# Turning merged rows from tokens to columns: transposes on TensorE, or 32x32 blocks on VectorE and a way through DRAM

## The chip, the cores and the metric

The kernel runs on one core of a Trainium2 chip. The metric is device time in microseconds (us) of one execution of the whole kernel, lower being better. The core has a matrix engine (TensorE, in the profile PE, with its weight loads as PEld), a vector engine (VectorE, DVE), a scalar engine (ScalarE, ACT), a general engine (GpSimd, POOL) and a queue that does little but issue transfers (SyncE, SP). The engines run side by side; each executes its own instructions strictly in the order in which the program emits them, and semaphores make one wait for another.

## What is computed

One layer of a bidirectional encoder: 256 tokens, width 2048, float32.

```python
xn = rms_norm(x, norm_pre_w)
u_lru, g_lru, q, k, v, g_attn, m_lru, m_attn = split(xn @ w_in)
y_a = (rg_lru forward + backward of the convolved u_lru) * silu(g_lru)
y_b = windowed_gqa(rope(q), rope(k), v, sink) * silu(g_attn)
merged = sigmoid(m_lru) * (y_a @ w_proj_a) + sigmoid(m_attn) * (y_b @ w_proj_b)
x = x + rms_norm(merged @ w_out, norm_post_w)
```

The last lines matter here. `merged` is 256 x 2048. The products that make it put tokens on the partitions; the product with `w_out` needs it the other way round, with `merged`'s columns on the partitions, because that is the dimension it sums over. Between the two, `merged` is turned.

## The kernel before

**Precision.** Each float32 operand is split into a high part (fp32r, made by a cast on ScalarE) and a low part (the remainder, made by a subtraction on VectorE), and a product is three matmuls: high by high, high by low, low by high. `split` does so for the weights (ScalarE L219, VectorE L221), `parts_of` for activations (ScalarE L148, and one tick later VectorE L149).

**Weights.** 1 MB of weights is one step: a *quad* (512 output columns by a quarter of the depth), a *block*, or a *part* of a Strassen-like scheme of seven products (class `Seven`; groups L, M, N, A and O). A quad has two halves of twelve matmuls each, a part two halves of six. The order of all steps is written out by hand in the strings `START`, `MERGE` and `OUT`. In `MERGE` the quads `b0.0` to `b3.3` are `y_b @ w_proj_b`, where the first digit is the column block c of 512 columns; in between stand parts of groups A and O. A raw load (SP, L207) goes to one of three ring buffers and is emitted three steps ahead of its matmuls; the cast is emitted four halves ahead and the subtraction three.

**Ticks.** Time in the program's text is counted in ticks: one for each half of a quad and one for a whole part. `soon(fn, d)` puts work d ticks later into the emission order; `at(tick, fn)` puts it at a given tick. Within a tick come the transfers that the step fetches, then the work that is due, then the splits, then the matmuls. So a load that waits on SP, or a subtraction that waits on VectorE, holds up all that was emitted behind it on the same engine.

**The turn.** `add_pb(c)` adds the four quads of column block c. One tick after the last of them `done` runs for both token halves: VectorE multiplies by the gate and adds the other branch (L977, L978), four operations in all. Then `turn(0)` and `turn(1)` (`turn(i)` takes 256 of the 512 columns) follow one and three ticks later. Each has four TensorE transposes of 128x128 into a PSUM bank (L989), a split of the turned bank into the tile `ms` (L148, L149), and `sums_of`, which makes the four sums and differences that the seven-product scheme needs into `mx` (L318 to L326, and another split). `ms` and `mx` are what the `o` quads and the O parts multiply with `w_out`.

**An older turn of the same kind.** The attention probabilities are already turned without TensorE: `head.flip` transposes 32x32 blocks on VectorE (L905), `head.send` writes four groups of 32 partitions to a DRAM tile `turn` with four transfers on SP (L914), and `head.fetch` reads it back with the partition groups in their places (L919), two ticks after the send.

**Memory.** Nearly all tiles are 4 KB per partition and come from one pool of 45 units; a new tile waits until its slot has been left by the tile before.

Of the kernel before, what the change touches and what calls it, by code (L numbers as in the profile page):

```python
# [15 lines left out]
F32 = mybir.dt.float32  # L16
F32R = mybir.dt.float32r
AF = mybir.ActivationFunctionType
ALU = mybir.AluOpType
PSUM = bass.MemoryType.PSUM  # L20

P = 128
# [80 lines left out]
def content(p):  # L103
    if p[0] == "part":
        _, g, a, q = p
        m, c = SEVENS[g]
        b, f = SEVEN[a][2]
        return "part", m, c + (-512 if g == "A" else 512) * f, b, q
    return p


def wall_rows():
    return {k: n for n, k in enumerate(dict.fromkeys(content(p) for p in load_plan()))}


def body(ctx, tc, x, x0, xT, wall, wlru, pvec, npost, ident_d, mask_d, rope_d, out):
    nc = tc.nc
# [5 lines left out]
    dram = ctx.enter_context(tc.tile_pool(name="dram", bufs=1, space=bass.MemoryType.DRAM))  # L123
    ctx.enter_context(tc.manual_schedule())

    def unit(name, dt=F32, shape=(P, 4, S)):
        return units.tile(list(shape), dt, tag="u", name=name)

    def bank(name, shape=(P, 2, S)):
        return psum.tile(list(shape), F32, tag="bg", name=name, bufs=4)  # L130
# [4 lines left out]
    def half_unit(name, tag, dt=F32, bufs=2):  # L135
        return small.tile([P, 2, S], dt, tag=tag, name=name, bufs=bufs)


    def pair_unit(name):
        return unit(name, F32R, (P, 2, 2, S))  # L140
# [6 lines left out]
    def parts_of(h, l, src):  # L147
        nc.scalar.copy(h, src)  # L148
        soon(lambda: nc.vector.tensor_tensor(l, src, h.bitcast(F32), ALU.subtract))  # L149
# [9 lines left out]
    def ticks(i=None):  # L159
        return sum(1 if p[0] == "part" else 2 for p in plan[:len(steps) if i is None else i])  # L160

    def at(hs, fn):
        assert hs >= now[0], (hs, now[0])
        due.setdefault(hs, []).append(fn)
# [9 lines left out]
    def soon(fn, d=1):  # L174
        at(now[0] + d, fn)
# [3 lines left out]
    row = wall_rows()  # L179
    flat = lambda t: t.rearrange("p a b -> p (a b)") if len(t.shape) == 3 else t  # L180

    def raw_tile(i):
        t = ring.tile([P, 2, 1024], F32, tag="raw", name=f"raw{i}", bufs=3)
        raws[i] = [t[:, h] for h in range(2)]
        return t
# [12 lines left out]
    def chained(i):  # L198
        return plan[i][0] == "part" and groups[plan[i][1]].where(plan[i][2]) != "z"

    def fetch(i, lead):
        if i >= len(plan):
            return
        if plan[i][0] == "part":
            groups[plan[i][1]].fetch(plan[i], lead)
        if lead == 3 and i not in raws and not chained(i):
            nc.sync.dma_start(flat(raw_tile(i)), wall[row[content(plan[i])]])  # L207
# [54 lines left out]
    def add_rows(name, act, done, spare=False, last=False):  # L262


        got, held = [], []

        def products(t, g, h, wh, wl):

            for low in range(2):
                for j in range(2):  # L270
                    k = 4 * g + 2 * h + j
                    sl = slice(j * 512, (j + 1) * 512)
                    a = act[k // 2][:, k % 2, :, t * P:(t + 1) * P]
                    for i in range(1 if low else 2):
                        nc.tensor.matmul(got[t], a[:, i], (wl if low else wh)[:, sl], start=k + low + i == 0, stop=low == 1 and k == KT - 1)  # L275

        def half(g, h, wh, wl):
            if g == 0 and h == 0:
                if last:
                    got.extend(banks(f"{name}{t}", (P, 2, 512))[:, 0] for t in range(2))  # L280
                elif spare:
                    got.extend(bank(f"{name}{t}", (P, 512)) for t in range(2))
                else:
                    ps = banks(name, (P, 2, 512))
                    got.extend(ps[:, t] for t in range(2))
            if last and g >= 2:
                products(0, g, h, wh, wl)
                held.append((1, g, h, wh, wl))
            else:
                for t in range(2):  # L290
                    products(t, g, h, wh, wl)
            if g == 3 and h == 1:
                if last:
                    done(0, got[0])
                    for a in held:
                        products(*a)
                    done(1, got[1])
                else:
                    soon(lambda: [done(t, got[t]) for t in range(2)])

        for g in range(4):
            steps.append(("quad", lambda h, wh, wl, g=g: half(g, h, wh, wl)))
# [6 lines left out]
    def sums_of(name, src, done, f=None):  # L309
        a = src.rearrange("p a b -> p (a b)")  # L310
        a11, a12, a21 = (a[:, i * P:(i + 1) * P] for i in (0, 2, 1))
        ends = src.rearrange("p a (b c) -> p (a b) c", b=2)[:, 0:4:3]
        psum = f is None
        f = (half_unit(f"{name}f", "uu", F32) if psum else f).rearrange("p a (b c) -> p (a b) c", b=2)
        t = unit(name, F32R, (P, 4, 2, P))

        def make(a21):
            nc.vector.tensor_tensor(f[:, 0:2], ends, a21.unsqueeze(1).to_broadcast([P, 2, P]), ALU.subtract)  # L318
            nc.vector.scalar_tensor_tensor(f[:, 2], f[:, 1], -1.0, a11, ALU.mult, ALU.subtract)
            nc.vector.scalar_tensor_tensor(f[:, 3], f[:, 2], -1.0, a12, ALU.mult, ALU.subtract)  # L320
            soon(lambda: parts_of(t[:, :, 0], t[:, :, 1], f))
            done(t)

        if psum:

            nc.scalar.copy(f[:, 3], a21)  # L326
            soon(lambda: make(f[:, 3]))
        else:
            make(a21)

    away = [dram.tile([P, 4, 4, 2 * P], F32, name=f"away{q}") for q in range(2)]

    def x_sums(n):
        v = unit(f"xa{n}")
        nc.vector.tensor_tensor(v[:, 0:2], xs[n][:, :, 0].bitcast(F32), xs[n][:, :, 1].bitcast(F32), ALU.add)
        store = lambda t: nc.sync.dma_start(away[n // 4][:, :, n % 4], t.rearrange("p a b c -> p a (b c)").bitcast(F32))
        sums_of(f"xx{n}", v[:, 0:2], lambda t: soon(lambda: store(t), 7), v[:, 2:4])
# [6 lines left out]
    class Seven:  # L346
# [42 lines left out]
        def rows(self, m, q, j):  # L389
            a, n = SEVEN[m][0], 4 * q + j  # L390
            if a[0] == "a":
                t, b = int(a[1]) - 1, int(a[2]) - 1
                src = self.act[n][:, b, :, t * P:(t + 1) * P]
            elif self.sums is None:
                src = self.kept[m, q][:, j]
            else:
                src = self.sums[n][:, SUMS.index(a)]
            return src[:, 0], src[:, 1]
# [355 lines left out]
    tm, sm, ms, msum = {}, {}, {}, {}  # L754
# [219 lines left out]
    def add_pb(c):  # L974
        def done(t, ps):
            g = sm[c][:, t]
            nc.vector.tensor_tensor(g, ps, g, ALU.mult)  # L977
            nc.vector.tensor_tensor(g, tm[c][:, t], g, ALU.add)  # L978
            if t == 1:
                for i in range(2):  # L980
                    soon(lambda i=i: turn(i), 1 + i * (1 if c == 3 else 2))

        def turn(i):

            ps = bank(f"mt{c}{i}")
            for t in range(2):
                for j in range(2):
                    sl = slice((2 * i + j) * P, (2 * i + j + 1) * P)
                    nc.tensor.transpose(ps[:, j, t * P:(t + 1) * P], sm[c][:, t, sl], ident)  # L989
            n = 2 * c + i  # L990
            m = ms[n] = pair_unit(f"ms{n}")
            parts_of(m[:, :, 0], m[:, :, 1], ps)
            sums_of(f"mx{n}", ps, lambda t: msum.update({n: t}))

        add_rows(f"pb{c}_", yb, done)
# [81 lines left out]
    b, n = ticks(), ticks(len(plan))  # L1077
# [159 lines left out]
```

## Time and profile before

| | us |
|---|---|
| median of 3 runs | 877.22 |
| lowest and highest | 876.87, 877.27 |
| the profiled execution | 876.5 |
| its span, first to last instruction | 874.7 |
| TensorE busy in the span | 864.9 |
| VectorE busy | 728.6 |
| ScalarE busy | 643.1 |

The profile is of one execution. Busy time is the time in which an engine executes; a wait is idle time just before an instruction, with the event that ended it. "L" and a number is a line of the kernel. A DMA row tells from the issue on the queue to the landing of the data. Positions are us from the start of the span, and a row of the timeline gives the start, the duration, the engine, the line, and in brackets the idle time before it.

### The profile page before, as it was taken

Reading aid. Unit: us, or ns where it says so; the run is one execution under the profiler, and the core shown is the slowest. Engines: PE = TensorE matmul, PEld = TensorE weight load, DVE = VectorE, ACT = ScalarE, POOL = GpSimd, SP = SyncE. Lnnn points to the kernel's source line nnn. Section 1 sums busy time; section 2 is a strip of 40 time slices with the busy share of each in tenths; the row PEclk is TensorE's granted clock in tenths of the full one; section 3 lists DMA queues with packets and bytes.
Section 4 is the critical chain, followed back from the end, with each engine's and each line's share of the span. In section 5 each row is a group of like instructions: output and inputs, shape, how many; then the busy total and the mean of one; then the engine's idle time right before and its main releaser. Section 6 shows DMA issues by size and latency. Waiting matters only on the chain.

```text
span 874.7 us, 12312 instructions
## 1 busy us (share of the span) xinstructions
PE 864.9 (99%) x4474; PEld 741.7 (85%) x4474; DVE 728.6 (83%) x975; ACT 643.1 (74%) x929; POOL 66.1 (8%) x97
## 2 busy tenths in 40 slices
PE   9999999999999999999999999999999999999996
PEld 8888888888888888888888888888888888888885
DVE  6898999898887989779677788988678778778885
ACT  7689687877888696887777699976567456555654
POOL 0000001012000011100001200000000101000200
PEclk9999999999999999999999999999999999999999
DMA  9757699999959999996999987999989988968772
GB/s 332 276 194 236 202 362 244 361 332 291 336 186 278 319 298 316 302 314 230 277 345 305 303 297 218 333 326 309 303 323 364 297 269 261 315 248 353 188 198 96
DMA packets 63390, 247.92 MB, mean 283 GB/s; under 512 B 6241, under 2 KB 19297, under 8 KB 47841
## 3 DMA queue, kind: packets, MB, share of 16 engines
q1 hardware_dynamic: 52384, 208.59, 64.6%
q0 software_dynamic: 10368, 37.75, 22.2%
q10 hardware_dynamic: 576, 0.79, 0.3%
q8 instruction: 35, 0.57, 0.2%
q14 instruction: 27, 0.21, 0.1%
HBM read 228.24 MB, written 18.87 MB: 283 GB/s over the span
## 4 chain that ended last, share of the span: by engine, by line
PE 94%; issue 3%; DMA 2%; ACT 0%; POOLq 0%; DVE 0%; SPq 0%; ACTq 0%
PE ga L255 7%; PE q L255 7%; PE gl L255 7%; PE u L255 5%; PE Am L410 4%; PE Mm L410 4%; PE Lm L410 4%; PE Nm L410 4%; PE ga L253 3%; PE q L253 3%; PE gl L253 3%; PE Om L410 3%; PE u L253 3%; PE pa__6025 L275 2%; PE pa__5514 L275 2%
## 5 line engine op out<-in xcount | busy, mean ns | idle before, releaser
L221 DVE TENSOR_TENSOR wl<-raw,wh 128x1024 fp32r<-128x1024 f32 (+1 forms) x252 | 299.1, 1203 | 56.5 <-ACT wh L219 43.9
L219 ACT CAST wh<-raw 128x1024 fp32r<-128x1024 f32 (+1 forms) x251 | 253.7, 1036 | 67.5 <-DMA raw<-wall_dram 39.6
L255 PE MATMUL ga<-xs,wh 128*128 128x512 f32 x256 | 63.5, 391 | 0.0
L255 PE MATMUL gl<-xs,wh 128*128 128x512 f32 x256 | 63.4, 391 | 0.0
L255 PE MATMUL q<-xs,wh 128*128 128x512 f32 x256 | 63.2, 391 | 0.0
L255 PEld LDWEIGHTS q<-xs,wh 128*128 128x128 f32 x256 | 47.0, 188 | 9.1
L255 PEld LDWEIGHTS gl<-xs,wh 128*128 128x128 f32 x256 | 47.0, 188 | 9.0
L255 PEld LDWEIGHTS ga<-xs,wh 128*128 128x128 f32 x256 | 46.7, 188 | 8.8
L255 PE MATMUL u<-xs,wh 128*128 128x512 f32 x192 | 47.5, 391 | 0.0
L255 PEld LDWEIGHTS u<-xs,wh 128*128 128x128 f32 x192 | 35.2, 188 | 6.7
L253 PEld LDWEIGHTS q<-xs,wl 128*128 128x128 f32 x256 | 33.2, 191 | 1.2
L253 PE MATMUL q<-xs,wl 128*128 128x256 f32 x256 | 34.0, 283 | 0.0
L253 PEld LDWEIGHTS ga<-xs,wl 128*128 128x128 f32 x256 | 33.0, 191 | 1.2
L253 PEld LDWEIGHTS gl<-xs,wl 128*128 128x128 f32 x256 | 32.8, 191 | 1.2
L253 PE MATMUL ga<-xs,wl 128*128 128x256 f32 x256 | 33.5, 283 | 0.0
L253 PE MATMUL gl<-xs,wl 128*128 128x256 f32 x256 | 33.2, 283 | 0.0
L253 PEld LDWEIGHTS u<-xs,wl 128*128 128x128 f32 x192 | 24.6, 191 | 0.9
L253 PE MATMUL u<-xs,wl 128*128 128x256 f32 x192 | 24.9, 283 | 0.0
L662 DVE SCALAR_TENSOR_TENSOR uu<-upad,pv,uu 128x256 f32<-128x256 f32 x48 | 23.2, 483 | 1.7
L746 ACT ACTIVATE sig<-sg 128x512 f32<-128x512 f32 x16 | 10.2, 635 | 14.1 <-DVE sg L589 14.1
L148 ACT CAST ms<-mt 128x512 fp32r<-128x512 f32 x8 | 4.7, 588 | 20.0 <-PE mt L989 20.0
L230 PE MATMUL gate<-ul,lwl 128*128 128x256 f32 x64 | 18.1, 283 | 0.0
(513 smaller groups left out, 2097.5 us busy)
## 6 DMA issues: line engine op xcount, KB each, us to landing
raw<-wall_dram SPq DMA_DIRECT2D x121, 1024.0 KB, 7.9
lraw<-wlru_dram SPq DMA_DIRECT2D x8, 512.0 KB, 6.3
away<-xx SPq DMA_DIRECT2D x8, 512.0 KB, 8.7
Lm<-away SPq DMA_DIRECT2D x8, 512.0 KB, 11.2
Mm<-away SPq DMA_DIRECT2D x8, 512.0 KB, 13.4
Nm<-away SPq DMA_DIRECT2D x8, 512.0 KB, 14.2
turn<-pt SPq DMA_DIRECT2D x32, 128.0 KB, 4.4
pl<-turn SPq DMA_DIRECT2D x8, 512.0 KB, 7.2
```

The costliest lines, as they stand in the source:

```text
L148: nc.scalar.copy(h, src)
L219: cast(hs, raw)
L221: nc.vector.tensor_tensor(ls, raw, hs.bitcast(F32), ALU.subtract)
L230: nc.tensor.matmul(ps, wl, xh, start=False, stop=stop, skip_group_check=more)
L253: nc.tensor.matmul(ps[:, 1], wl[:, sl], a[:, 0], start=False, stop=False)
L255: nc.tensor.matmul(ps, wh[:, sl], a, start=k == 0, stop=k == KT - 1)
L275: nc.tensor.matmul(got[t], a[:, i], (wl if low else wh)[:, sl], start=k + low + i == 0, stop=low == 1 and k == KT - 1)
L410: nc.tensor.matmul(self.ps[b], a[i], (wl if low else wh)[:, sl], start=fresh and j + low + i == 0, stop=last and j + low == 2, skip_group_ ...
L662: nc.vector.scalar_tensor_tensor(u, up[:, j, tap:tap + S], cw[:, tap:tap + 1], u, ALU.mult, ALU.add)
L746: nc.scalar.activation(sg, dst, AF.Sigmoid)
```

## The change

For column blocks 0, 1 and 2 the turn takes another way; block 3 keeps the transposes, at the delays it had. One tick after `done`, `flip` lets VectorE transpose the merged tile (128 x 1024) in 32x32 blocks. One tick on, `send` issues four transfers on SP, each for 32 partitions, into a DRAM tile. Three ticks after the flip `fetch` reads that tile back, 512 KB, with the partition groups exchanged. Six and seven ticks after the flip, `rows(0)` and `rows(1)` make from it what `turn(0)` and `turn(1)` made: the split into `ms`, and the sums into `mx` by a new function, which takes its operands from the fetched tile in SBUF and needs no copy of `a21`, but four VectorE operations in place of three.

```diff
+    def turned_sums_of(name, src, done):
+
+        f = half_unit(f"{name}f", "uu", F32).rearrange("p a (b c) -> p (a b) c", b=2)
+        t = unit(name, F32R, (P, 4, 2, P))
+        row = [f[:, i].rearrange("p (a x) -> p a x", a=4) for i in range(4)]
+        a11, a21, a12, a22 = (src[:, i // 2, 4 * (i % 2):4 * (i % 2) + 4] for i in range(4))
+        nc.vector.tensor_tensor(row[0], a11, a21, ALU.subtract)
+        nc.vector.tensor_tensor(row[1], a22, a21, ALU.subtract)
+        nc.vector.scalar_tensor_tensor(row[2], row[1], -1.0, a11, ALU.mult, ALU.subtract)
+        nc.vector.scalar_tensor_tensor(row[3], row[2], -1.0, a12, ALU.mult, ALU.subtract)
+        soon(lambda: parts_of(t[:, :, 0], t[:, :, 1], f))
+        done(t)
...
-            if t == 1:
+            if t == 1 and c == 3:
                 for i in range(2):
-                    soon(lambda i=i: turn(i), 1 + i * (1 if c == 3 else 2))
+                    soon(lambda i=i: turn(i), 1 + i)
+            elif t == 1:
+                soon(flip)
+
+        v = {}
+
+        def flip():
+            v["t"] = unit(f"mt{c}", F32, (P, 2, 4, 4, 32))
+            nc.vector.transpose(v["t"].rearrange("p t c k x -> p t k c x"), sm[c].rearrange("p t (k c x) -> p t k c x", k=4, c=4))
+            for d, fn in enumerate((send, None, fetch, None, None, lambda: rows(0), lambda: rows(1)), 1):
+                if fn:
+                    soon(fn, d)
+
+        def send():
+            v["d"] = dram.tile([4, 32, 2, 4, P], F32, name=f"turnm{c}")
+            t = v.pop("t")
+            for a in range(4):
+                nc.sync.dma_start(v["d"][:, :, :, a].rearrange("c i t x -> i t c x"),
+                                  t[a * 32:(a + 1) * 32].rearrange("p t c k x -> p t c (k x)"))
+
+        def fetch():
+            v["u"] = unit(f"mu{c}", F32, (P, 1024))
+            nc.sync.dma_start(v["u"], v["d"].rearrange("c i t a x -> (c i) (t a x)"))
+
+        def rows(i):
+            src = v["u"].rearrange("p (a k x) -> p k a x", a=8, k=4)[:, 2 * i:2 * i + 2]
+            n = 2 * c + i
+            m = ms[n] = pair_unit(f"ms{n}")
+            wide = lambda s: m[:, :, s].rearrange("p k (a x) -> p k a x", a=8)
+            parts_of(wide(0), wide(1), src)
+            turned_sums_of(f"mx{n}", src, lambda t: msum.update({n: t}))
```

## The prediction

> **What bounds the kernel now.** First the page: who is busy, and who stands in the chain that ended last.
>
> ```profile
> PE 864.9 (99%) x4474; PEld 741.7 (85%) x4474; DVE 728.6 (83%) x975; ACT 643.1 (74%) x929; POOL 66.1 (8%) x97
> PE 94%; issue 3%; DMA 2%; ACT 0%; POOLq 0%; DVE 0%; SPq 0%; ACTq 0%
> ```
>
> TensorE is busy throughout and holds 94% of the chain; 99% alone proves little, since ends of matmuls are modelled. So next the chain in order of time, around the turns of column blocks 0, 1 and 2 ("rounds" below).
>
> ```profile
> 696.48 2.72 PE Am L410 x12
> 699.76 5.48 PE pb__6872 L275 x24
> 705.67 2.77 PE Am L410 x12
> 708.44 10.88 PE pb__6872 L275 x48
> ...
> 727.48 2.72 PE Am L410 x12
> 730.76 5.48 PE pb__7124 L275 x24
> 736.67 5.49 PE pb__7124 L275 x24
> 742.16 2.72 PE Am L410 x12
> ...
> 758.48 2.72 PE pb__7337 L275 x12
> 761.76 2.76 PE pb__7337 L275 x12
> 764.51 2.72 PE Am L410 x12
> 767.67 2.77 PE Om L410 x12
> 770.44 5.44 PE pb__7337 L275 x24
> ```
>
> Twelve matmuls take 2.72 us wherever no turn lies between, and the next group starts where the last ended: a tick is 2.72 us, and TensorE waits for nobody. Only the transposes break the pace. From 696.48 to 708.44 are 11.96 us for 48 matmuls, which the row after does in 10.88: 1.08 us. From 727.48 to 742.16 are 14.68 for 60, by the pace 13.60: 1.08. From 758.48 to 770.44 are 11.96 for 48: 1.08. This is what a round's two turns cost the bound engine.
>
> **TensorE's part.** The change takes 24 of 32 transposes from TensorE.
>
> ```profile
> L989 PE MATMUL mt<-ident,sm x16: 270/272/329, 699.0 to 736.4; 128*128 128x128 f32 x16
> L148 ACT CAST ms<-mt x8: 587/588/588, 699.8 to 796.0; 128x512 fp32r<-128x512 f32 x8
> L149 DVE TENSOR_TENSOR ms<-mt,ms x8: 683/684/685, 702.6 to 797.2; 128x512 fp32r<-128x512 f32 x8
> L326 ACT COPY mx0f<-mt x1: 270/270/270, 700.3 to 700.3; 128x128 f32<-128x128 f32 x1
> L318 DVE TENSOR_TENSOR mx0f<-mt,mx0f x1: 415/415/415, 703.2 to 703.2; 128x256 f32<-128x256 f32 x1
> L319 DVE SCALAR_TENSOR_TENSOR mx0f<-mx0f,mt x1: 286/286/286, 703.6 to 703.6; 128x128 f32<-128x128 f32 x1
> ```
>
> I take 3 x 1.08 = 3.24 us, from starts in the chain, not 24 x 0.272 = 6.53 us, the durations: those overlap, and the pace is what the successor feels. [...]
>
> **ScalarE and VectorE, the same work from another place.** A round loses two copies L326 on ScalarE (0.54 us); the casts of the new `rows` are 128x512 as before, so 0.588 each; reading runs of 32 elements is not in the trace and lies between that and a doubling. It costs nothing while ScalarE idles (12.3 us of 20 busy, below). On VectorE the three operations of the sums (0.415, 0.286 and another of 0.286: 0.99) become four of 128x128: 4 x 0.286 = 1.14, at most 4 x 0.415 = 1.66. The remainders L149 stay. New is the flip.
>
> ```profile
> L905 DVE STREAM_TRANSPOSE pt<-p x16: 704/706/712, 516.7 to 646.6; 128x512 f32<-128x512 f32 x16
> L914 SPq DMA_DIRECT2D turn<-pt x32: 575/611/1465, 524.7 to 649.2; - x32
> DMA to landing us min/median/max: 2.5/4.4/9.4
> L919 SPq DMA_DIRECT2D pl<-turn x8: 319/326/327, 530.4 to 657.9; - x8
> DMA to landing us min/median/max: 3.2/7.2/9.3
> ...
> 720.00:740.00 20.00, 20.00 (x93) 16.42 (x93) 17.20 (x24) 12.28 (x16) 3.50 (x4) 1.00 0.77 230
> ```
>
> The flip is twice as wide: 2 x 0.706 = 1.41 us. A round so adds to VectorE 1.41 + 2 x 0.15 = 1.7 us, and 5.1 in all. In the 20 us of the last row VectorE is busy 17.2; it keeps 2.8 in hand there, so by sums this fits. By order it is tighter.
>
> **Round 0: when must the fetch land?**
>
> ```profile
> 701.45 1.22 DVE L221 TENSOR_TENSOR wl<-Ax0b,wh 128x1024 fp32r<-128x1024 f32 x1
> ...
> 716.70 1.23 DVE L221 TENSOR_TENSOR wl<-raw,wh 128x1024 fp32r<-128x1024 f32 x1 [1.32 <-issue]
> ...
> 727.52 0.69 DVE L977 TENSOR_TENSOR sm<-pb__6872,sm 128x512 f32<-128x512 f32 x1 [2.05 <-PE pb__6872 L275]
> 730.18 3.49 DVE L221 TENSOR_TENSOR wl<-raw,wh 128x1024 fp32r<-128x1024 f32 x3
> ```
>
> The flip comes in front of the split at 701.45, the third after `done`, so it ends at 702.9. Four sends at 0.61 put the last issue at 704.7; by the medians it lands 4.4 later, and the fetch 7.2 after that: 716.4. `rows(0)` stands six ticks behind the flip, the tick of the split at 716.70, before which VectorE already idled 1.32: it arrives at 715.4 and stops there until the data are in. Behind it, up to the next `done`, are five low splits (6.1), two sets of sums (2.3), four remainders (2.7) and one combine of part results (0.7): 11.8 us. Then come the four merging operations (2.8) and the low split of b2.0's second half (1.22). TensorE needs that half at 730.76 - 0.56 (transposes: 727.48 + 2.72 to 730.76) - 1.08 + 2.72 + 0.9 (four high matmuls first) = 732.7. Back from there: landing by 716.9. By the medians 0.5 us are in hand; with both maxima (9.4 + 9.3) it is 723.4 and 6.5 late; with both minima 710. I take zero, as the nearest rows are transfers of just this shape and their medians.
>
> **Round 1: the weight loads behind the sends.** On SP, sends and fetch stand between weight loads.
>
> ```profile
> 697.42 0.33 SPq L809 DMA_DIRECT2D sm<-parksm  x1
> 700.42 0.33 SPq L207 DMA_DIRECT2D raw<-wall_dram  x1
> ...
> 727.48 6.55 SPq L207 DMA_DIRECT2D raw<-wall_dram  x3
> ...
> 747.65 5.49 SPq L207 DMA_DIRECT2D raw<-wall_dram  x3
> ...
> DMA to landing us min/median/max: 6.2/10.2/12.9
> ```
>
> The last line is the landing of the three loads at 727.48. They are b2.2, b2.3 and b3.0; the sends go behind the first, the fetch before the second. The flip starts at 730.18 + 2 x 1.16 - 1.08 = 731.4 and ends at 732.8, the last send is issued at 734.7, it lands at 739.1, the fetch goes out, and b2.3 follows at 739.6 instead of about 731. Landed: 749.8 by the 10.2 us of this stretch, which is DMA-busy. b2.3 starts on TensorE at 742.16 - 2.16 + 2.72 + 5.44 + 2.72 = 750.9; with 0.9 as above, and cast (1.04) and split (1.22) before it:
>
> ```profile
> L219 ACT CAST wh<-raw 128x1024 fp32r<-128x1024 f32 (+1 forms) x251 | 253.7, 1036 | 67.5 <-DMA raw<-wall_dram 39.6
> raw<-wall_dram SPq DMA_DIRECT2D x121, 1024.0 KB, 7.9
> ```
>
> needed by 749.5. So 0.3 late by the local median, 2.0 early by the median of all 121 loads (7.9), 3.7 early by the minimum, and with the slowest send and the slowest load (+5.0, +2.7) 8.0 late. I take 0.3.
>
> **Round 2, round 0's loads, and the rest.** In round 2 the sends stand before b3.2's load, the third of those at 747.65. The merge starts at 758.48 - 2.16, the flip ends four operations (2.75), a split (1.22) and 1.41 later at 761.7, the sends are issued by 764.2, then the load, landing at 772.1 by 7.9 or 774.4 by 10.2. b3.2 starts three steps after 767.67, at 778.6 - 3.24 = 775.4, so 774.0 is early enough: between 1.9 in hand and 0.4 late; I take zero, since the sends are then all that waits on SP. In round 0 the load at 700.42 goes out after the sends, at about 705.5; it feeds b1.3, on TensorE at 719.32 + 2.72 - 1.08 = 721.0, so it has 15 us. POOL's accumulating load into Ax0b waits for the split behind the flip: 1.4 us later, for data that Am4.0 takes, ten steps after the part that freed the tile. The two new tiles per round take two of 45 slots, and the four they replace are allocated six ticks later. What TensorE no longer writes, no bank of PSUM has to hold. If these covers are gone, each costs what lands late, one for one.
>
> **Sum.** -3.24 + 0.3 = -2.9 us. The profiled execution took 876.5 (span 874.7 and 1.8 around it) and would take 873.6; it stands 0.7 below the median of the runs, 877.2, so I predict 874.3.
>
> **Rivals.**
> - *The way through DRAM is slow (slower).* b2.3's load waits on SP for the sends' landing, and TensorE waits for b2.3. For: the loads of this stretch took 10.2 in the median, and a send up to 9.4. At the far end 8.0 late: 877.2 - 3.24 + 8.0 = 882.0. It decides from a landing of b2.3 at 749.5 + 3.24 + 1.75 = 754.5 on. Against: by the 7.9 us of all loads b2.3 is 2.0 early, and each wait on SP also leaves the DMA engines more room for what follows. Chance 0.24. [...]
> - *The gain is eaten on VectorE (within 0.2%).* Round 0's fetch lands 1.5 to 5 us after 716.9, and the backlog of 11.8 us reaches TensorE. For: only 0.5 in hand. Against: 2.05 us of idle time before L977. Around 3 late: 877.0. Chance 0.22.
> - *TensorE was not the bound.* Then its holes stay where the transposes were: 877.2. For: weight loads are only 85% busy. [...] Against: the even pace of 2.72 us. Chance 0.04.
>
> **How the numbers follow.** My forecast, a stall of at most 1.5 us in all, has 0.50: 873.8 to 875.5. A kernel within 0.2% (1.75 us) can't be told from no change: faster 0.50, same 0.26 (the second and third rival), slower 0.24. The range of 8 in 10 leaves out half a tenth below 873.5 (less than no stall) and the worst of the slower cases, stalls beyond 6 us: 873.5 to 880.0.
>
> **What the profile of the changed kernel would show.** Right: in the chain, 2.72 us per twelve matmuls without a break from 690 to 789; flips of about 1.4 us; the fetched tiles landing by 716.9 in round 0, b2.3's load by 749.5 in round 1; TensorE with no idle time before a `pb` or Am matmul. Wrong: casts that wait for raw loads, or TensorE waiting for low splits in 715 to 760; or an earlier stage with the same end, which would mean that something in the O stage sets the end. The prediction fails if transfers land slower than their medians in rounds 0 and 1, for there the margins are 0.5 and -0.3 us.

## The result, and the profile after

The changed kernel takes 883.46 us in the median of six runs (881.61 to 884.08), against 877.2 for the kernel before on the same chip: a ratio of 1.0069, 95% interval 1.0056 to 1.0082. It is slower by 6 us where 2.9 less was forecast, and it lies beyond the upper end of the range. The profiled execution took 883.3 us, with a span of 881.6 (before: 874.7).

First the page of the changed kernel: busy times, the engines' shares of the chain that ended last, and the group of ScalarE's casts of weights.

```profile
PE 866.1 (98%) x4450; PEld 741.8 (84%) x4450; DVE 732.1 (83%) x984; ACT 642.2 (73%) x923; POOL 66.1 (7%) x97
...
PE 87%; DMA 5%; DVE 3%; issue 3%; ACT 1%; SPq 0%; POOLq 0%; ACTq 0%; DVEq 0%
...
L219 ACT CAST wh<-raw 128x1024 fp32r<-128x1024 f32 (+1 forms) x251 | 253.8, 1035 | 89.4 <-DMA raw<-wall_dram 59.5
```

The 24 transposes are gone (4474 - 4450), and yet TensorE is not done sooner. Its share of the chain fell from 94% to 87%, and DMA and VectorE took the place. The last row says what came late: of the 89.4 us for which ScalarE stood before a cast of weights, 59.5 were ended by a raw load. The chain in order of time (start, duration, what) shows where:

```profile
735.12 2.12 PE pb__7115 L275 x8
...
737.28 0.09 DVE mt L1002
...
739.50 9.82 DMA turnm<-mt
749.37 0.33 SPq L1016
...
749.80 5.45 DMA raw<-wall_dram
...
755.35 1.05 ACT wh L219
...
756.45 8.52 PE pb__7115 L275 x24
764.97 5.45 PE pb__7335 L275 x24
...
775.03 9.98 DMA raw<-wall_dram
...
798.43 0.70 DVE mg L991
...
799.17 0.44 PE mt L1032 x2
```

Up to 727 the chain stays with TensorE; from there to 735 it runs through VectorE's splits and merges, late out of round 0. Then it runs through round 1 as the rival "the way through DRAM is slow" has it: flip, sends, landing of the sends, fetch, and only then the load of b2.3, its cast, and TensorE. Behind it stand 24 matmuls that take 8.52 us, and the next 24 take 5.45. Further on the chain leaves TensorE again: VectorE's splits at 770, a raw load at 775.03 that goes out behind them, its cast, more work of VectorE. It comes back to TensorE at the transposes of block 3, which wait for the merge on VectorE (L991).

The table of stretches of 20 us shows the same two places (busy time of PE, PEld, DVE, ACT and POOL, then the granted clock, the share of the DMA engines and GB/s):

```profile
740.00:760.00 20.00, 17.10 (x68) 13.74 (x67) 10.55 (x17) 7.24 (x10) 0.87 (x1) 0.89 0.90 265
760.00:780.00 20.00, 20.00 (x85) 16.46 (x84) 17.67 (x20) 11.68 (x14) 1.73 (x2) 0.94 0.95 274
780.00:800.00 20.00, 18.87 (x85) 15.21 (x84) 15.72 (x24) 9.70 (x13) 0.00 (x0) 1.00 1.02 419
```

Before, TensorE had 90 to 93 matmuls in each of these stretches, at a clock of 1.00. After, it has 68 from 740 to 760, with 2.9 us idle, and the granted clock falls to 0.89 and 0.94; from 756 to 762 it is 0.50. So this stall cost twice: TensorE stood, and it then ran at half clock. TensorE's own timeline at that place:

```profile
756.45 2.08 PE L275 MATMUL pb__7115<-wh,yb 128*128 128x512 f32 x4 [2.90 <-ACT wh L219]
...
759.17 1.91 PE L275 MATMUL pb__7115<-wh,yb 128*128 128x512 f32 x4
...
763.44 1.07 PE L275 MATMUL pb__7115<-wh,yb 128*128 128x512 f32 x4
```

Four matmuls take 1.91 where they take 1.07 a little later. The 24 matmuls at 756.45 took 8.52 instead of 5.45: 3.1 us lost on top of the stall of 2.9. With 1.1 us in round 0 and 1.3 at block 3's transposes, TensorE loses 8.4 us after 690. Less the 3.24 us that the transposes cost no longer, 5.2 are explained of the 6.9 by which the two spans differ; about 1.0 of the rest is there before the change begins: the part of group A that started at 696.48 starts at 697.46. That is scatter: in the profiled executions of the kernels here, which do the same work up to there, the first matmul of this part starts anywhere from 696.0 to 697.8.

Last SP's own timeline, which holds what the rest of this document turns on (start, duration to the end of the last of the group, line, and the count):

```profile
703.69 4.14 SPq L1011 DMA_DIRECT2D turnm<-mt  x4
707.95 1.98 SPq L207 DMA_DIRECT2D raw<-wall_dram  x1
...
714.90 0.32 SPq L1016 DMA_DIRECT2D mu<-turnm  x1
...
737.39 2.77 SPq L1011 DMA_DIRECT2D turnm<-mt  x4
749.37 0.33 SPq L1016 DMA_DIRECT2D mu<-turnm  x1
749.80 0.85 SPq L207 DMA_DIRECT2D raw<-wall_dram  x2
...
770.77 2.55 SPq L1011 DMA_DIRECT2D turnm<-mt  x4
773.42 0.56 SPq L207 DMA_DIRECT2D raw<-wall_dram  x1
```

In each round a weight load goes out right behind the sends or the fetch. The loads that the kernel before issued at 700.42, about 731 and about 753 go out at 707.95, 749.80 and 773.42.

### The profile page after: what moved, and what is told of

It reads as the page before. It is cut to its first block, busy times and chain, and to the rows that moved or that the text cites. A ratio compares the mean times of both kernels' runs of the same rounds, so it can differ in the third digit from the quotient of the medians.

```text
span 881.6 us, 12291 instructions
## 1 busy us (share of the span) xinstructions
PE 866.1 (98%) x4450; PEld 741.8 (84%) x4450; DVE 732.1 (83%) x984; ACT 642.2 (73%) x923; POOL 66.1 (7%) x97
## 4 chain that ended last, share of the span: by engine, by line
PE 87%; DMA 5%; DVE 3%; issue 3%; ACT 1%; SPq 0%; POOLq 0%; ACTq 0%; DVEq 0%
PE ga L255 7%; PE q L255 7%; PE gl L255 7%; PE u L255 5%; PE Mm L423 4%; PE Lm L423 4%; PE Nm L423 4%; PE gl L253 3%; PE ga L253 3%; PE q L253 3%; PE Am L423 3%; DMA raw<-wall_dram 3%; PE Om L423 3%; PE u L253 3%; PE pa__5770 L275 2%
## 5 line engine op out<-in xcount | busy, mean ns | idle before, releaser
L219 ACT CAST wh<-raw 128x1024 fp32r<-128x1024 f32 (+1 forms) x251 | 253.8, 1035 | 89.4 <-DMA raw<-wall_dram 59.5
L275 PE MATMUL pb__7115<-wh,yb 128*128 128x512 f32 x64 | 19.4, 429 | 2.9 <-ACT wh L219 2.9
L759 ACT ACTIVATE sig<-sg 128x512 f32<-128x512 f32 x16 | 10.2, 637 | 14.2 <-DVE sg L602 14.2
L275 PEld LDWEIGHTS pb__7115<-wh,yb 128*128 128x128 f32 x64 | 13.5, 212 | 6.3 <-ACT wh L219 3.3
```

The source lines that it names most:

```text
L219: cast(hs, raw)
L759: nc.scalar.activation(sg, dst, AF.Sigmoid)
```

## The experiments

Each run is compared with the kernel before on its own chip, whose medians were 876.8 to 877.4. Differences in the text are of medians as they stand, so between two chips they hold to some 0.6 us. Letters are theories: A, SP waits for the landing of the sends and holds b2.3's load; B, the added traffic; C, VectorE's added work; D, the sends' small packets; G, VectorE stands until the fetch has landed; H, SP stands until the flip is done and holds every load behind.

| run | us (low to high) | ratio to before (95%) |
|---|---|---|
| e1 no turn at all | 874.12 (872.72 to 874.58) | 0.9966 (0.9953, 0.9978) |
| e2 fetch doesn't wait | 882.48 (881.35 to 883.35) | 1.0063 (1.0051, 1.0076) |
| e3 later fetch in round 1 | 882.3 (882.12 to 884.09) | 1.0066 (1.0052, 1.0080) |
| e4 round 1 alone | 881.83 (881.31 to 883.41) | 1.0059 (1.0047, 1.0072) |
| e5 packets of 4 KB | 881.35 (879.46 to 882.0) | 1.0044 (1.0032, 1.0056) |
| e6 sends on ScalarE's queue | 882.61 (880.48 to 882.92) | 1.0058 (1.0046, 1.0070) |
| e7 rounds 0 and 2 alone | 881.07 (878.85 to 882.94) | 1.0048 (1.0033, 1.0063) |
| e8 TensorE kept busy | 883.33 (882.89 to 885.42) | 1.0076 (1.0064, 1.0088) |
| e9 flips alone | 873.6 (873.49 to 874.35) | 0.9960 (0.9947, 0.9972) |
| e10 flips and sends | 880.89 (880.18 to 882.76) | 1.0046 (1.0033, 1.0058) |
| e11 flips and fetches | 873.29 (872.75 to 874.13) | 0.9955 (0.9943, 0.9967) |
| e12 later rows | 881.66 (879.9 to 882.44) | 1.0048 (1.0034, 1.0062) |
| e13 sends of 8 KB | 877.13 (874.36 to 878.79) | 1.0000 (0.9991, 1.0009) |
| e14 sends that wait for nothing | 874.84 (873.17 to 875.54) | 0.9975 (0.9967, 0.9984) |
| e15 sends behind the loads | 879.96 (879.34 to 880.85) | 1.0038 (1.0025, 1.0052) |
| e16 GpSimd's queue | 888.69 (887.7 to 889.79) | 1.0139 (1.0125, 1.0153) |
| e17 placed by round | 876.57 (875.45 to 878.7) | 1.0000 (0.9991, 1.0009) |
| e18 two rounds placed | 875.97 (875.02 to 876.32) | 0.9987 (0.9978, 0.9996) |

### Is there a gain, and does the named wait eat it? (e1 to e4)

**e1**: no flip, send or fetch; the rows read the merged tile as it is, so it isn't turned at all.

```diff
+            v["u"] = flat(sm[c])
+            soon(lambda: rows(0), 6)
+            soon(lambda: rows(1), 7)
```

> Column blocks 0 to 2 are not turned at all: rows() reads the merged tile as it lies (so those rows of the product with w_out are made from unturned data); flip, sends and fetch are left out. This prices the 24 transposes alone. If TensorE's pace was the bound, 877.2 - 3.24 = 874.0 us, within 0.6. If TensorE was not the bound, 877.2.

874.12, 2.65 below its before, with the interval reaching from 1.9 to 4.1 less. TensorE has no idle time before a matmul from 690 to 855. TensorE's part of the forecast, 3.24 us, is within this.

**e2**: the fetch reads an older DRAM tile, so it waits for no send and brings other data.

```diff
-            nc.sync.dma_start(v["u"], v["d"].rearrange("c i t a x -> (c i) (t a x)"))
+            nc.sync.dma_start(v["u"], away[0][:, 0].rearrange("p a x -> p (a x)"))
```

> The fetch reads 512 KB of another DRAM tile that was written long before (so the turned data are not used), at the same place on SP: flips, sends, bytes and packets stay, only the wait of SP for the landing of the sends goes. Theory A (weight loads are held up behind the fetch on SP; TensorE then idles 3.1 us and is slowed 3.1 us by its clock): 883.5 - 6.2 = 877.3, or up to 1.3 less if round 0's stall goes too; no half clock. Theory B (the added DMA traffic itself delays the loads): 883.5, within 1. Theory C (VectorE's added work): 883.5, within 1.

882.48, hardly better. b2.3's load went out at 739.75 and landed at 752.63, 12.9 us later; TensorE stood 2.18 us before that weight, and 2.05 and 0.89 at block 3's transposes. Theory A, my first rival as the prediction put it, falls as the sole cause.

**e3**: in round 1 the fetch is emitted two ticks later, behind b2.3's load, and the rows two ticks later as well.

```diff
+            late = (None, None) if c == 1 else ()
-            for d, fn in enumerate((send, None, fetch, ...
+            for d, fn in enumerate((send, None, *late, fetch, ...
```

> In round 1 alone the fetch comes five ticks behind the flip in place of three, behind the loads of b2.3 and b3.0 on SP, and rows() two ticks later; all data right, same traffic, same work. Theory A: 883.5 - 6.2 = 877.3, within 1, no half clock. Theory B and theory C: 883.5, within 1.

882.3. The stall of round 1 is gone, and the time stays: TensorE now stood 1.21 us at 769.24, and 2.01 and 0.89 at block 3's transposes. A repair in one place moved the loss to another.

**e4**: only block 1 takes the new way.

```diff
-            if t == 1 and c == 3:
+            if t == 1 and c != 1:
                 for i in range(2):
-                    soon(lambda i=i: turn(i), 1 + i)
+                    soon(lambda i=i: turn(i), 1 + i * (1 if c == 3 else 2))
```

> Only round 1 goes through DRAM; blocks 0, 2 and 3 use TensorE's transposes at their old ticks. Theory A: round 1 has nearly the whole loss: 877.2 - 1.1 + 6.2 = 882.3, within 1.2. Theories B and C, by which each round costs alike: 877.2 + 6.3 / 3 = 879.3.

881.83: one round alone, with a gain of 1.08 to offer, makes nearly the whole loss.

### Packets, queue, rounds, clock (e5 to e8)

**e5**: each send writes its 32 partitions in pieces of 4 KB rather than 512 B; the partition groups are then not exchanged.

```diff
-                nc.sync.dma_start(v["d"][:, :, :, a].rearrange("c i t x -> i t c x"),
-                                  t[a * 32:(a + 1) * 32].rearrange("p t c k x -> p t c (k x)"))
+                nc.sync.dma_start(v["d"].rearrange("c i t a x -> (c i) (t a x)")[a * 32:(a + 1) * 32],
+                                  t[a * 32:(a + 1) * 32].rearrange("p t c k x -> p (t c k x)"))
```

> Theory A fell: without the wait for the landing, and with the fetch behind the loads, the sends still took about 10 us and b2.3's load, behind them in the queue, landed just as late. [...] Here the sends write the same bytes by the same four transfers, but each partition's 4 KB as one piece (the partition groups are not exchanged, so the data are not turned fully). Theory D: round 1's sends land within 6 us, no half clock in 745 to 765, about 877 us (875.5 to 879). Theory B (the added bytes): 882.5 to 883.5, sends still about 10 us.

881.35, about 2 us better than the changed kernel. The sends of round 1 still landed 7 to 9 us after their issue. Piece size is a part of it at most.

**e6**: the sends go out on ScalarE's queue, with e3's later fetch.

```diff
-                nc.sync.dma_start(v["d"][:, :, :, a]...
+                nc.scalar.dma_start(v["d"][:, :, :, a]...
```

> The sends go out on ScalarE's queue, the fetch of round 1 five ticks behind the flip as in e3_late_fetch1; data right, same pieces. Theory D: the sends are as slow as before in round 1, but no load stands behind them, and in round 2 b3.2's load no longer waits for the flip: stalls of rounds 1 and 2 go, ScalarE loses 2.4 us a round to the issues where it has slack: 876 us (874.5 to 878). Theory B: 882 to 883.5.

882.61. No load of SP stands behind the sends themselves now, but the fetch and the loads behind it still wait for the landing, and the last send of round 1 landed 16.7 us after its issue. VectorE stood for the fetch, with splits behind it, and TensorE waited for one of these; VectorE's row and TensorE's:

```profile
759.17 0.29 DVE L341 TENSOR_TENSOR mx2f<-mu 128x128 f32<-128x128 f32 x1 [6.27 <-DMA mu<-turnm]
```

```profile
769.30 0.72 PE L423 MATMUL Am<-wl,xs 128*128 128x512 f32 x2 [3.18 <-DVE wl L221]
```

In round 2 ScalarE stood at the sends until the flip was done, with a cast of weights behind it, for which TensorE stood 0.60 us at 774.86. Another queue brought other waits, and the time stayed.

**e7**: blocks 0 and 2 take the new way, block 1 the transposes (e4's edit with `c in (1, 3)`).

> Rounds 0 and 2 go through DRAM; blocks 1 and 3 use transposes at their old ticks. If the losses of the rounds add up: the whole change lost 6.3, round 1 alone 5.1, so 877.2 + 1.2 = 878.4, within 1.5. If the rounds stand for each other's backlog (each alone enough to make the later stage late): 881 or more.

881.07. e4 and e7 together hold each round once. Against the no-turn level of 874.1 plus 1.08 for each round on TensorE, e4 loses 5.5 and e7 5.9: 11.4 together, where all three rounds in one kernel lose 9.4. The losses don't add. My reading, which no run tests by itself, is that each round ends up holding back work that the next round needs.

**e8**: twelve matmuls that nothing uses, at the tick of b2.3, so that TensorE doesn't idle there.

```diff
+    def fill():
+        ps = bank("fill", (P, 512))
+        for _ in range(12):
+            nc.tensor.matmul(ps[:, 0:P], ones, ones, start=True, stop=True)
+
+    at(tick["b2.3"], fill)
```

> The changed kernel with twelve unused float32 matmuls (24 passes, some 2.8 us) ahead of b2.3, where TensorE idled 2.9 us for b2.3's cast; they write a bank that nobody reads. If the half clock after the stall comes from the idling, TensorE stays at full clock, b2.3 takes 5.4 us in place of 8.5: 883.5 - 3 = 880.5. If the slow matmuls have another cause (the DMA traffic), 883.5 or, with the added work, more.

883.33, no change. The stall there shrank to 0.53 us and no half clock followed it (granted clock 1.00 from 740 to 780), but a stall of 1.58 and 0.82 us came up at block 3's transposes, with half clock behind that (0.94 in the mean from 780 to 800). With TensorE kept at work the half clock left that place, and the time stayed: the work that TensorE waits for was late all the same.

### Which part costs it? (e9 to e12)

**e9** flips alone, **e10** flips and sends, **e11** flips and fetches; the rows read the flipped tile (in e11 the fetched one).

```diff
-            for d, fn in enumerate((send, None, fetch, None, None, lambda: rows(0), lambda: rows(1)), 1):
+            for d, fn in enumerate((send, None, None, None, None, lambda: rows(0), lambda: rows(1)), 1):
...
-            src = v["u"].rearrange("p (a k x) -> p k a x", a=8, k=4)[:, 2 * i:2 * i + 2]
+            src = v["t"].rearrange("p t c k x -> p k (t c) x")[:, 2 * i:2 * i + 2]
```

This is e10's edit; e9 leaves the send out as well, and e11 has the fetch without the send, from an older tile as in e2.

> Flips, row splits and sums as in the changed kernel, without sends and without the fetch; the rows read the flipped tile, whose partition groups are then not exchanged. Before at 877.0, the run without turns at 874.1. Theory C (VectorE's added work, three flips of 1.24 us, makes the loss): 880 or more. Theories B, D and G (the transfers, or the wait for them): 874.1 plus at most 1, about 874.5; TensorE then has no stall and no half clock.

> Flips and sends, no fetch; the rows read the flipped tile, so no engine waits for a landing and SP waits only for the flip. The exchange between partition groups is left out. Theory G (VectorE standing still before rows(0) until the fetch has landed makes most of the loss): about 875. Theories B and D (the added transfers in a stretch of full DMA engines, and b2.3's load in the same queue behind them): 877 to 881, with b2.3's load landing after 751.

> Flips and fetches, no sends: each fetch reads 512 KB of an older DRAM tile, so SP waits for no landing, and the rows read what it brings (not the merged rows). Theory A or D (the four small-piece sends and SP's wait for them): the loss is gone, 874.5 to 875.5. Theory B (any added transfer): 876 to 878. Theory G: about 875, since the fetch lands before rows(0), unless it is itself slow.

873.6, 880.89 and 873.29. This was the clearest answer of the study: VectorE's flips and split rows cost nothing (C falls), 512 KB a round through a fetch cost nothing (B falls), and the sends alone cost 7.3 us, although nobody waits for their landing (G falls as the main cause). SP's timeline of e9 first, and of e10 second:

```profile
726.65 7.66 SPq L207 DMA_DIRECT2D raw<-wall_dram  x3
...
743.93 9.70 SPq L207 DMA_DIRECT2D raw<-wall_dram  x3
```

```profile
733.90 3.17 SPq L1011 DMA_DIRECT2D turnm<-mt  x4
737.17 1.28 SPq L207 DMA_DIRECT2D raw<-wall_dram  x2
...
744.27 11.51 SPq L207 DMA_DIRECT2D raw<-wall_dram  x2
765.76 2.56 SPq L1011 DMA_DIRECT2D turnm<-mt  x4
768.41 0.55 SPq L207 DMA_DIRECT2D raw<-wall_dram  x1
```

In e9 the third of the loads at 743.93, b3.2's, goes out at 753.3. In e10 it goes out at 768.41: SP reaches the sends of round 2 after 755.8 and stands there until VectorE has done the flip at 765.7, and the load, which needs nothing of the flip, stands behind. What it leads to, in VectorE's and TensorE's timelines of e10:

```profile
774.90 2.36 DVE L221 TENSOR_TENSOR wl<-raw,wh 128x1024 fp32r<-128x1024 f32 x2 [2.39 <-ACT wh L219]
781.23 1.23 DVE L221 TENSOR_TENSOR wl<-raw,wh 128x1024 fp32r<-128x1024 f32 x1 [3.98 <-ACT wh L219]
...
793.49 0.69 DVE L991 TENSOR_TENSOR mg<-tm,mg 128x512 f32<-128x512 f32 x1
```

```profile
792.91 0.44 PE L1032 MATMUL mt<-ident,mg 128*128 128x128 f32 x2 [2.14 <-DVE mg L991]
794.24 0.44 PE L1032 MATMUL mt<-ident,mg 128*128 128x128 f32 x2 [0.89 <-DVE mg L991]
```

Late loads make late casts, VectorE stands 2.39 and 3.98 us for them, and the merge of block 3, which stands behind those splits, ends at 794.2. In e9 its first operation waited 4.92 us for TensorE instead:

```profile
786.51 0.69 DVE L990 TENSOR_TENSOR mg<-pb__7321,mg 128x512 f32<-128x512 f32 x1 [4.92 <-PE pb__7321 L275]
```

**e12**: rows nine and ten ticks behind the flip, rather than six and seven.

> The changed kernel with rows(0) and rows(1) nine and ten ticks behind the flip rather than six and seven; all data as in the changed kernel. Theory G: VectorE no longer stands 8.0 and 5.6 us before the sums of rounds 0 and 1, and the time falls to about 877 or below, with b2.3's late load still costing some 3. Theory of the transfers alone: unchanged, 882 to 883.5.

881.66: 1.8 us of the loss go with VectorE's idle time before the sums, the rest stays. TensorE stood 1.39 us at 752.12 for b2.3's cast, 1.03 at 768.32 for a split, and 2.04 and 0.89 before block 3's transposes.

### The wait, or the bytes? (e13, e14)

**e13**: as e10, but two partitions of each 32 are sent. **e14**: as e10, but what is sent is a tile written long before; by its edit the rows read the flipped tile, as in e10, and not the tile that is sent, as its expectation has it.

```diff
-                nc.sync.dma_start(v["d"][:, :, :, a].rearrange("c i t x -> i t c x"),
-                                  t[a * 32:(a + 1) * 32].rearrange("p t c k x -> p t c (k x)"))
+                nc.sync.dma_start(v["d"][:, 0:2, :, a].rearrange("c i t x -> i t c x"),
+                                  t[a * 32:a * 32 + 2].rearrange("p t c k x -> p t c (k x)"))
```

```diff
-            t = v.pop("t")
+            t = yb[0].rearrange("p a b s -> p (a b s)").bitcast(F32).rearrange("p (t c k x) -> p t c k x", t=2, c=4, k=4)
```

> As the run with sends alone, but each send carries two partitions (8 KB) instead of 32 (128 KB): the wait of SP for the flip stays, the transferred bytes are nearly gone. The rows read the flipped tile, and the exchange between partition groups is left out. Theory H (SP's wait for the flip): the loss stays, 879 to 881, and the load of b3.2 goes out at about 766 rather than 753. Theory D (the packets of the sends): 873.6 to 874.5.

> As the run with sends alone, but the sends carry 512 KB of a tile that was written long before (a tile of y_b), in the same pieces: SP doesn't wait for the flip. The rows read that tile too, so neither the merged rows nor their exchange are in the output. Theory H: no loss, 873.6 to 875. Theory D: the loss stays, 879 to 881.

877.13 and 874.84. Over the flips alone (873.6) the wait without the bytes costs 3.5 us, the bytes without the wait 1.2, and both together 7.3, which is 2.6 more than their sum (the intervals of e9 and e14 touch, those of e9 and e13 lie apart). e9 and e10 ran on another chip than e13 and e14; each taken against the kernel before on its own chip, the wait costs 4.0, the bytes 1.75, both 7.3, and 1.5 is left over. Neither theory had its number: H comes out larger than D, and together they cost more than each by itself. SP's timeline of e13, then of e14:

```profile
763.53 2.56 SPq L1011 DMA_DIRECT2D turnm<-mt  x4
766.19 0.34 SPq L207 DMA_DIRECT2D raw<-wall_dram  x1
```

```profile
755.41 3.32 SPq L1011 DMA_DIRECT2D turnm<-yb  x4
758.84 3.84 SPq L207 DMA_DIRECT2D raw<-wall_dram  x1
```

With the wait, b3.2's load goes out at 766.19, as forecast. Without it, at 758.84, behind sends that went out at once. One thing is not held fixed: e14's sends leave 5 to 10 us earlier than e10's, so its 1.2 us price the bytes at another moment. The wait for the flip is spent on the queue that issues, as the rows of e10 and e13 show: SP issues nothing between 755.8 and 765.7 in e10, and nothing between 753.6 and 763.5 in e13.

### Another place for the sends (e15 to e18)

**e15**: send five ticks behind the flip, fetch seven, rows nine and ten, with all data as in the changed kernel.

```diff
-            for d, fn in enumerate((send, None, fetch, None, None, lambda: rows(0), lambda: rows(1)), 1):
-                if fn:
-                    soon(fn, d)
+            for d, fn in ((5, send), (7, fetch), (9, lambda: rows(0)), (10, lambda: rows(1))):
+                soon(fn, d)
```

> The changed kernel with its data right, but send five ticks after the flip rather than one, fetch seven rather than three, rows nine and ten rather than six and seven: by the order of SP's instructions b1.3's, b2.3's, b3.2's and b3.3's loads are then ahead of the sends, and the flip is done when SP comes to them. Theory H: 874 to 877, faster than before or the same, since what is left is only the wait of the fetch. Theory D: 879 to 882.

879.96, a number of theory D's range. Up to 765 TensorE lost nothing, and in rounds 0 and 1 the gain was there. Round 2 gave it back, by a wait of another kind. VectorE's timeline, then TensorE's:

```profile
787.62 0.29 DVE L341 TENSOR_TENSOR mx4f<-mu 128x128 f32<-128x128 f32 x1 [7.06 <-DMA mu<-turnm]
```

```profile
792.94 0.69 PE L1031 MATMUL mt<-ident,mg 128*128 128x128 f32 x2 [2.61 <-DVE mg L991]
794.27 0.69 PE L1031 MATMUL mt<-ident,mg 128*128 128x128 f32 x2 [0.64 <-DVE mg L991]
```

The fetch of round 2 stood behind the loads of x on SP and landed at 787.6; VectorE reached `rows(0)` 7.06 us earlier and stood, with block 3's merge behind. Behind the stall TensorE ran at half clock for 6.8 us (granted clock 0.83 in the mean from 780 to 800).

**e16**: e12's ticks with sends and fetch on GpSimd's queue.

```diff
-                nc.sync.dma_start(v["d"][:, :, :, a]...
+                nc.gpsimd.dma_start(v["d"][:, :, :, a]...
...
-            nc.sync.dma_start(v["u"], v["d"]...
+            nc.gpsimd.dma_start(v["u"], v["d"]...
```

> The changed kernel with sends and fetch issued by GpSimd, one and three ticks after the flip, rows nine and ten ticks after it: no weight load of SP stands behind them, but the accumulating loads of groups A and O on GpSimd do. Theory H: 874 to 877, unless an accumulating load comes late. Theory D: the packets still pass the same DMA engines, though in another queue, 877 to 881.

888.69, the slowest of all. GpSimd stood at the sends, and the accumulating loads behind came late, as the expectation allowed for. TensorE stood 6.18 us at 768.55, and the mean granted clock of the run was 0.988, against 0.997 or 0.998 in the runs of the kernel before. Two of the waits of e16:

```profile
POOL turnm L1010 <- DVE mt L1002: 100.0, 3, 82.0
ACT wh L219 <- DMA Ax1a<-wall_dram: 18.8, 1, 18.8
```

**e17**: e15's places in rounds 0 and 1; in round 2 send, fetch and rows at three, four, nine and ten. **e18**: e15's places in rounds 0 and 1; round 2 on TensorE.

```diff
+            for d, fn in zip(((5, 7, 9, 10), (5, 7, 9, 10), (3, 4, 9, 10))[c], (send, fetch, lambda: rows(0), lambda: rows(1))):
+                soon(fn, d)
```

> All data as in the changed kernel. Rounds 0 and 1: send, fetch, rows(0), rows(1) five, seven, nine and ten ticks after the flip; round 2: three, four, nine and ten, so that the fetch stands before the loads of x. Theory H (order on SP, and VectorE's wait for the fetch, make the loss): 873.5 to 876, with no stall of TensorE for block 3's merge. Theory D (the transfers themselves): 879 or more.

> Only blocks 0 and 1 by VectorE and DRAM, with five, seven, nine and ten ticks; blocks 2 and 3 by TensorE's transposes at the delays of the kernel before. Theory H: the two rounds keep their 2 x 1.08 us, 874.5 to 876. If it comes out at 877 or above, rounds 0 and 1 still cost something that no stall of TensorE before 790 shows.

876.57 and 875.97. Between e15 and e17 only round 2's send and fetch have moved, and 3.4 us came back, so it was the place of these transfers and not their bytes; between the changed kernel and e17 only ticks differ, and 6.9 of the 9.9 us above the flips alone came back (6.5 of 10.0, each against the kernel before on its own chip). The longest of TensorE's waits left in e17:

```profile
792.67 0.44 PE L1031 MATMUL mt<-ident,mg 128*128 128x128 f32 x2 [0.89 <-DVE mg L991]
```

e17 missed its expectation by 0.6 us at the upper end, e18 lies at the end of its own. e17 is even with the kernel before, though it issues 24 transposes fewer. e18 lies 0.13% below, with an interval that ends at 0.04% below: less than the 0.2% that I had set as the bound of what a measurement can tell. No version here that turns all of its data beats the kernel before by more than that.

## Why the prediction was wrong, point by point

**The step that failed** is the term for stalls. The sum has 0.3 us for it; TensorE lost 8.4. It was small for two reasons: the sends were priced by a median of 4.4 us from another stage, where the last sends of rounds 0 and 1 took 7.8 and 9.82 to land; and a load held up on SP was compared with its own deadline alone, which gave zero for rounds 0 and 2, where the runs show that everything behind the held load comes late. The signs of being wrong that the prediction names were there: slow landings in rounds 0 and 1, casts that waited for raw loads, and TensorE waiting for low splits at 731.34 and 735.12.

**TensorE's part held.** 3.24 us from starts in the chain; e1 gave 1.9 to 4.1, and the flips alone 2.5 to 4.7. By the durations of the transposes, 0.272 us each, it would have been 6.5, which both intervals exclude. The timelines agree: from the first matmul of the part of group A at 696 to the last two matmuls of the kernel are 169.78 us before and 166.54 with flips alone, 3.24 less.

**ScalarE and VectorE held.** The flip took 1.24 us (1.41 taken), the four sums 1.07 (1.14 taken), the casts from runs of 32 elements 0.61 (0.588 to twice that taken), and e9 shows that they cost nothing.

**Round 0 failed by the landing.** "I take zero, as the nearest rows are transfers of just this shape and their medians": the last send landed 7.8 us after its issue, not 4.4, and the data came at 720.4, not 716.4. Of these 4.0 us the flip made 0.8 and the issuing of the four sends, which took 4.14 us, another 1.5; the landing made 3.4, and the fetch, with 5.5 in place of 7.2, gave 1.7 back. In VectorE's timeline of the changed kernel:

```profile
702.43 1.24 DVE L1002 STREAM_TRANSPOSE mt<-sm 128x1024 f32<-128x1024 f32 x1
...
720.38 0.29 DVE L341 TENSOR_TENSOR mx0f<-mu 128x128 f32<-128x128 f32 x1 [8.01 <-DMA mu<-turnm]
```

VectorE stood 8.01 us, and TensorE waited for low splits at 731.34 and 735.12, 0.24 and 0.90 us. The second rival described this; its size was 1.1 us for TensorE, not 3, but the flip of round 1 came late behind it.

**Round 1 failed by the same term, and by one that wasn't there.** Its sends went out at 737.4 to 739.5 rather than up to 734.7, since the flip came late out of round 0, and they landed after 9.82 instead of 4.4. So b2.3's load was issued at 749.8, ten later than the sum has it. Landed it was at 755.25, against the 749.5 that it needed; the load itself took 5.45 and not 10.2, as the rival's own remark had it that a wait on SP leaves the DMA engines room (from 740 to 750 their busy share was 0.85, and 1.03 before). The half clock that follows the stall, 3.1 us, is in no term of the sum.

**Round 2 failed by what was counted.** "I take zero" compared the landing of b3.2's load with its own deadline. It landed at 778.6, and TensorE didn't wait for that weight. But behind late casts VectorE's splits stand, and behind these block 3's merge, for which four transposes on TensorE wait: 0.24 and 0.89 us in the changed kernel, 2.14 and 0.89 in e10. (The 3.4 us between e15 and e17 price the placing of this round too, but there the wait was for the fetch.)

**The slower rival had the right place and one wait of several.** It said 882.0 from a landing of b2.3 past 754.5; the load landed at 755.25, and TensorE's longest stall was for it. That its 8.0 us come near the 8.4 is luck: it has one stall there, and the 8.4 are 2.9 of stall and 3.1 of half clock in round 1, 1.1 in round 0 and 1.3 at block 3. And taking away the wait for the landing (e2), or the fetch from before the load (e3), gave back 1 us. What the runs showed beside it: SP stands at the sends already, until the flip is done (in round 2 of the changed kernel the flip ended at 770.7, and the first send went out at 770.77). The prediction wrote this delay down three times ("goes out after the sends" and "then the load, landing at 772.1" among them) and each time compared the load that was held with its deadline alone. The ring has three raw buffers, so a late load also means a late cast, a late split, and a later start of the loads behind it; the runs on single rounds show that this lasts beyond the round.

**Still open.** How the 1.5 to 2.6 us by which wait and bytes together exceed their sum come about. A part is the half clock: e10's profiled execution had 3.4 us of it (granted clock 0.83 in the mean from 790 to 800), which costs 1.7, and e13's and e14's had none; the rest isn't explained. Of the 3.4 us between the spans of e17 and of the flips alone, 1.3 lie before the change begins (the part of group A starts at 697.83 and at 696.55), and of the 2.1 behind it 1.6 are TensorE's waits against its pace.

## What to carry to other kernels

A transfer that waits for a computing engine, put on the queue that also issues loads, made every load behind it here into work that depends on that engine (in e10 b3.2's load went out at 768.41 rather than 753.3); price it by all that stands behind it, the casts, splits and merges of other engines included, and not by the next load's deadline alone. Put it where its data are ready by the time the queue arrives: the same instructions at other ticks were worth 6.9 us here. To tell a wait from its bytes, send few bytes with the wait, and then the same bytes without it.

## What was not expected of the hardware

**Half clock after a short stall.** After 2.90 us of idle TensorE the changed kernel ran at half clock for 6.8 us (granted clock 0.50 from 756 to 762), after 2.14 and 0.89 us e10 for 3.4 us (four matmuls in 1.75 and 1.72 us), after 1.58 and 0.82 us e8 for 3.4 us (1.74 and 1.72), after 2.19 us at 754.20 e4 for 3.4 us (the first four in 2.07 us); in their profiled executions e13 (1.43 and 0.89, then four matmuls in 1.18 and 1.09 us) and e5 (1.30 and 0.89, granted clock 1.00 from 780 to 800) kept the full clock. The length of the stall doesn't decide alone: e2 kept the full clock behind 2.18 us at 753.83 (granted clock 1.00 from 740 to 780), and e6 behind 3.18, 1.21 and 0.60 us from 769 to 775 (1.00 from 760 to 800). Nor does the program: of e13's eleven runs the five with a granted clock of 0.997 took 874.36 to 876.25, the six with 0.995 or 0.996 took 877.13 to 878.79, and 3.4 us at half clock are 0.002 of such a run's mean clock. So I estimate from these runs that a stall of this length is a risk of 1.7 us or more, half of 3.4, and not a fixed price. What decides beside the length, no run here shows.

**Small packets beside accumulating loads.** In round 1, while GpSimd's accumulating loads (queue 0) moved, the sends (queue 1) got a fifth of the DMA engines' time for more than twice as many packets. From 738 to 749 us of the changed kernel, then from 771 to 776, in round 2, where queue 0 is nearly still (packets, MB, share of 16 engines):

```profile
q0 software_dynamic: 460, 1.64, 76.0%
q1 hardware_dynamic: 1088, 0.52, 19.8%
```

```profile
q1 hardware_dynamic: 1127, 0.84, 75.5%
q0 software_dynamic: 23, 0.05, 5.6%
```

The same four sends landed 9.8 to 10.8 us after their issue in round 1 and 2.5 to 2.9 in round 2; with pieces of 4 KB (e5) it was 6.8 to 8.8 and 1.9 to 2.3, so the size of the pieces is not the whole of it. A median over another stage says little about such a transfer.
